# A feed-forward's products of halves: seven instead of eight, with the up-projection and the down-projection apart

## The chip, the cores and the metric

One core of a Trainium2 chip. The metric is the device time of one execution in microseconds (us); the time given for a kernel is the median of its runs.

The engines are named as in the profile: PE is TensorE (matmuls; PEld its weight loads), DVE is VectorE, ACT is ScalarE, POOL is GpSimd, SP is SyncE, which issues the DMAs. A suffix q (SPq) is an engine's own queue of DMA issues and waits.

## The reference

One layer of a streaming encoder, in float32, for 1024 tokens of a prompt and 64 tokens of a sample, 1088 columns in all: two kinds of attention, an attention into a memory, and a feed-forward with a short convolution. The change is in the feed-forward alone, and in the norm that feeds it:

```python
D_MODEL, D_FF, CONV_W = 1024, 2816, 3

def conv_ffn(h, prev, w_up, w_conv, b_conv, w_down):
    gu = h @ w_up                                   # 1024 -> 2 * 2816
    gate, val = gu[..., :D_FF], gu[..., D_FF:]
    t = gate.shape[1]
    gp = jnp.concatenate([prev.astype(gate.dtype), gate], axis=1)
    conv = sum(gp[:, j:j + t] * w_conv[j] for j in range(CONV_W)) + b_conv
    y = (jax.nn.silu(conv) * val) @ w_down          # 2816 -> 1024
    return y, gp[:, -(CONV_W - 1):]

xp = xp + mem_attend(rms_norm(xp, g_norm2), mk, mv, w_mq, g_mq, w_mo)
f, conv_p = conv_ffn(rms_norm(xp, g_norm3), zeros_prev, w_up, w_conv, b_conv, w_down)
xp = xp + f                                         # the same for the sample's xs
```

## The kernel before

All of it runs transposed: features lie on the 128 partitions, the 1088 tokens along the free axis. A float32 product is made of three matmuls: each operand is split in a high part (`hi`, a cast on ACT to a narrower float, fp32r) and a low part (`lo`, the operand less its high part, on POOL or DVE), and hi x hi, hi x lo and lo x hi are summed in PSUM (`SPLIT`).

Tokens come in three chunks (`CHUNKS`: 384, 384 and 320). `gemm` (L859) makes the products of one block of 128 outputs with one chunk in eight pieces, one for each 128 of the inner dimension, of three matmuls each (L866), in a PSUM bank named `pj`. The weights come through `Stream` (L831): halves of 128 x 512 are loaded to `raw` on SP (L840), cast to `hi` on ACT (L848) and `lo` made on POOL (L849).

The output of the memory attention goes through `project`, which adds it to the residual, stores the sum in DRAM (`x2d`, called `xd`), multiplies it by the next norm's gain into two parts (`h3`, in the slots `hhi` and `hlo`), and sums its squares; `after_mo` (its matmul is L1194) makes the reciprocal root of a chunk's mean square from those, `rstd`. It is applied behind the gate's and the value's products, and not to `h3`.

The feed-forward goes over 22 blocks of 128 features (`Tile`, L1235). `Tile.run` (L1258) makes the block's gate for the three chunks, times `rstd` on DVE into a padded row (L1269); the convolution is an ACT instruction (L1272) and two on DVE over 1090 columns (L1274), then SiLU on ACT (L1276) and `rstd` again on POOL (L1280). The value's products follow, times the gate on DVE (L1287), split in two parts on ACT (L1288) and POOL (L1289). Between the pieces of these products stand those of `Tile.down` (L1292) of the block before: for 8 blocks of outputs and 3 chunks, three matmuls each (L1298) in the banks `PT`, `O` and `tq`, added by DVE (L1305) into eight rows `y` in SBUF. The first block adds the residual (loaded at L1302), the last stores the result (L1307). The block's rows of the down-projection's weights are loaded (L1247) and split (L1255 on ACT, L1256 on POOL) in slots named `kPh` to `vSl`.

The tile framework's scheduler puts the instructions of each engine in an order and adds the waits; rows of a tile pool are reused when all readers of the earlier content are done.

Of the kernel before, what the change touches and what calls it, by code (L numbers as in the profile page):

```python
# [15 lines left out]
P = 128  # L16
# [17 lines left out]
CHUNKS = ((0, 384), (384, 384), (768, 320))  # L34


@with_exitstack
def hybrid_step(ctx: ExitStack, tc: tile.TileContext, i: dict, o: dict):
# [30 lines left out]
    def rsq(pl, ms, out, n, rows=P):  # L69
        """out = ms ** -0.5, by exp and log and one step of Newton's."""  # L70
# [8 lines left out]
    # ------------------------------------------------------------------ projections and attention  # L79
# [12 lines left out]
    ps = ctx.enter_context(tc.tile_pool(name="ps", bufs=1, space=PSUM))  # L92
# [58 lines left out]
    def load_x(c, z):  # L151
        """Half of the columns of 256 tokens, or of the sample's 64."""
# [45 lines left out]
    # K, V and Q of a pair of heads over 256 tokens  # L198
# [14 lines left out]
    def qk_norm(p, sq, raw, eps_ap, rows):  # L213
        """q and k of raw [rows, 256], each head's normed, twice in a row; k with its gain, for the cache."""
# [35 lines left out]
    def place(main, subs):  # L250
        """main, and after some of its parts others."""
# [6 lines left out]
    def proj(p, t, subs):  # L258
        """One block of tokens through a pair's columns, woven with subs; what is to be done with it later."""
# [79 lines left out]
    def forget():  # L339
        """log sigmoid of the forget logits, and their running sums."""  # L340
# [4 lines left out]
        # z = exp(-|f|); log1p(z) = log(u) - ((u - 1) - z) / u with u = 1 + z  # L345
# [1076 lines left out]
```

## Time and profile before

| | |
|---|---|
| median of 3 runs | 1879.69 us (1878.67 to 1885.91) |
| span of the profiled execution | 1878.9 us, 0.8 below the median |
| mean granted TensorE clock | 0.992 |
| PE busy | 1808.8 us, 96% of the span |
| weight loads busy | 1754.7 us, 93% |
| DVE, ACT, POOL busy | 1071.5 us (57%), 800.9 us (43%), 937.4 us (50%) |
| feed-forward, first to last matmul | 1091.7 to 1874.9 us |
| DMA over the span | 157.49 MB, 84 GB/s in the mean |

The rows of the profile read as follows. In a group, "x168 | 93.1, 554 | 92.3 <-PE PT L1298 92.3" is 168 instructions, 93.1 us busy in all, 554 ns in the mean for one, and 92.3 us for which the engine was idle just ahead of them, ended by PE's matmuls of L1298. In a row by source, "x24: 671/682/1785" is the shortest, the median and the longest in ns. A row of the timeline begins with the start and the duration in us. Matmuls overlap in the pipeline, so that the distance of two starts, not the duration, is what one more of them takes. DMA rows end with the KB of one and the median us from issue to landing; in the engines' tenths each digit is a fortieth of the span.

### The profile page before, as it was taken

The numbers are of one execution on the slowest core, as the hardware profiler recorded it, in microseconds if no ns is written. First come the engines' busy times: TensorE is split into PE (matmuls) and PEld (weight loads), VectorE is DVE, ScalarE is ACT, GpSimd is POOL, SyncE is SP. The second block draws the span as 40 slices with busy tenths as digits, with TensorE's granted clock in tenths as the row PEclk, the third lists the DMA queues.
The fourth block names the chain that finished last, engine by engine and source line by source line (L and its number), as shares of the span: only waits on it lengthen the run. The fifth ranks groups of instructions, "written<-read, shape, count | busy, mean of one in ns | idle before, by whom it ended". The sixth has DMA issues, their size and how long they took to land.

```text
span 1878.9 us, 31543 instructions
## 1 busy us (share of the span) xinstructions
PE 1808.8 (96%) x11426; PEld 1754.7 (93%) x11426; DVE 1071.5 (57%) x2537; ACT 800.9 (43%) x1828; POOL 937.4 (50%) x1312
## 2 busy tenths in 40 slices
PE   6899999999997899999999999999999999999999
PEld 5789999999996788999999999999999999999999
DVE  6777766767766875334443345445545545555546
ACT  5656666767766665335543332212212212222220
POOL 5646666877976443434433444434434434443441
PEclk9999999999998999999999999999999999999999
DMA  8312122212216776421113433111111111111102
GB/s 276 89 45 68 43 76 77 63 55 76 60 34 177 248 227 196 144 67 52 60 52 122 137 104 106 45 40 51 40 45 51 35 51 45 40 51 40 45 23 97
DMA packets 111339, 157.49 MB, mean 84 GB/s; under 512 B 15480, under 2 KB 75000, under 8 KB 111184
## 3 DMA queue, kind: packets, MB, share of 16 engines
q1 hardware_dynamic: 111184, 155.48, 26.6%
q8 instruction: 90, 1.47, 0.3%
q14 instruction: 65, 0.53, 0.1%
HBM read 125.40 MB, written 33.18 MB: 84 GB/s over the span
## 4 chain that ended last, share of the span: by engine, by line
PE 54%; POOL 1%; issue 1%; ACT 0%; DVE 0%; POOLq 0%; DVEq 0%; ACTq 0%
PE pj L866 37%; PE PT L1298 7%; PE tq L1298 3%; PE O L1298 3%; PE S L1110 1%; PE O L1146 1%; PE tq L1146 1%; POOL lo L849 1%; PE PT L1133 0%; PE O L1110 0%; PE PT L1091 0%; POOL s L1125 0%; PE PT L1194 0%; ACT hi L848 0%; PE PT L1026 0%
## 5 line engine op out<-in xcount | busy, mean ns | idle before, releaser
L866 PE MATMUL pj<-hhi,hi 128*128 128x384 f32 (+1 forms) x1248 | 412.8, 331 | 0.0
L866 PE MATMUL pj<-hlo,hi 128*128 128x384 f32 (+1 forms) x1248 | 408.8, 328 | 0.0
L866 PE MATMUL pj<-hhi,lo 128*128 128x384 f32 (+1 forms) x1248 | 408.3, 327 | 0.0
L849 POOL TENSOR_TENSOR lo<-raw,hi 128x512 fp32r<-128x512 f32 x136 | 176.9, 1302 | 336.7 <-ACT hi L848 336.0
L848 ACT CAST hi<-raw 128x512 fp32r<-128x512 f32 x136 | 84.1, 620 | 406.5 <-issue 253.0
L866 PEld LDWEIGHTS pj<-hhi,hi 128*128 128x128 f32 x1248 | 234.5, 188 | 0.5
L866 PEld LDWEIGHTS pj<-hlo,hi 128*128 128x128 f32 x1248 | 234.6, 188 | 0.1
L866 PEld LDWEIGHTS pj<-hhi,lo 128*128 128x128 f32 x1248 | 234.4, 188 | 0.1
L1305 DVE TENSOR_TENSOR a<-PT,a 128x384 f32<-128x384 f32 (+1 forms) x252 | 133.9, 531 | 158.2 <-PE PT L1298 158.2
L268 PE MATMUL pj<-whi,xhi 128*128 128x384 f32 (+1 forms) x512 | 195.5, 382 | 7.9 <-ACT xhi L126 6.7
L866 PE MATMUL pj<-a,hi 128*128 128x384 f32 (+1 forms) x736 | 183.5, 331 | 3.6 <-DVE qhi L1001 1.7
L268 PE MATMUL pj<-whi,xlo 128*128 128x384 f32 (+1 forms) x512 | 175.7, 343 | 5.9 <-DVE xlo L127 5.9
L268 PE MATMUL pj<-wlo,xhi 128*128 128x384 f32 (+1 forms) x512 | 177.2, 346 | 2.9 <-POOL wlo L119 2.9
L866 PEld LDWEIGHTS pj<-a,hi 128*128 128x128 f32 x736 | 129.4, 188 | 6.2 <-DVE a L909 2.5
L454 ACT ACTIVATE s<-s,mx 128x640 f32<-128x640 f32 (+7 forms) x128 | 94.2, 736 | 79.1 <-DVE mx L452 77.5
L491 DVE TENSOR_TENSOR ptl<-PT,pth 128x512 fp32r<-128x512 f32 (+2 forms) x192 | 99.6, 522 | 38.8 <-ACT pth L490 36.5
L866 PE MATMUL pj<-a,lo 128*128 128x384 f32 (+1 forms) x368 | 120.7, 329 | 0.0
L220 POOL TENSOR_TENSOR r<-m,mhalf 128x4 f32<-128x4 f32 (+1 forms) x72 | 73.8, 1025 | 90.0 <-DVE m L219 80.0
L268 PEld LDWEIGHTS pj<-whi,xhi 128*128 128x128 f32 x512 | 100.0, 196 | 8.9 <-ACT xhi L126 6.7
L268 PEld LDWEIGHTS pj<-whi,xlo 128*128 128x128 f32 x512 | 98.0, 191 | 6.6 <-DVE xlo L127 6.6
L268 PEld LDWEIGHTS pj<-wlo,xhi 128*128 128x128 f32 x512 | 99.6, 195 | 4.5 <-POOL wlo L119 4.5
L490 ACT CAST pth<-PT 128x512 fp32r<-128x512 f32 (+2 forms) x192 | 85.1, 449 | 38.2 <-PE PT L489 36.8
(443 smaller groups left out, 4465.2 us busy)
## 6 DMA issues: line engine op xcount, KB each, us to landing
raw<-in_w_up_dram SPq DMA_DIRECT2D x88, 256.0 KB, 2.6
kvraw<-in_w_down_dram SPq DMA_DIRECT2D x44, 256.0 KB, 2.5
wraw<-in_w_dram SPq DMA_DIRECT2D x56, 192.0 KB, 2.4
mwraw<-in_w_mkv_dram SPq DMA_DIRECT2D x16, 512.0 KB, 5.6
s<-in_xn_dram SPq DMA_DIRECT2D x8, 512.0 KB, 6.8
mixd<-mix SPq DMA_DIRECT2D x32, 128.0 KB, 1.8
bias<-negc SPq DMA_DIRECT2D x8, 512.0 KB, 3.6
raw<-in_w_o_dram SPq DMA_DIRECT2D x16, 256.0 KB, 3.5
```

Source lines behind the costliest of these rows:

```text
L220: pool.tensor_tensor(r[:rows], m[:rows], mhalf[:rows, 0:4], op=ALU.pow)
L268: pe.matmul(pj[:, :nw], x2[a][:, k, t * P:(t + 1) * P], wt[k][b][:, :nw], start=n == 0, stop=n == 3 * KT - 1)
L454: act.activation(s[:, :n], s[:, :n], ACT.Exp, bias=mx, scale=-1.0, accum_out=sm)
L490: act.copy(hi[:, f:f + n, j], pt[:, f:f + n])
L491: dve.tensor_tensor(lo[:, f:f + n, j], pt[:, f:f + n], f32(hi[:, f:f + n, j]), op=ALU.subtract)
L848: act.copy(hi, raw)
L849: pool.tensor_tensor(lo, raw, f32(hi), op=ALU.subtract)
L866: pe.matmul(out()[:, :cn], w[a][:, k % 4], x[b][k][:, c0:c0 + cn], start=k == 0 and n == 0, stop=k == KT - 1 and n == 2)
L1110: pe.matmul(sp[:rows], self.q[a][:, d, t * P:t * P + rows], k[b][:, d], start=n == 0, stop=n == 5)
L1146: pe.matmul(op[:, a0:a1], v[x][:, b, d * P:(d + 1) * P], self.p2[y][:, b, a0:a1], start=n == 0, stop=n == 5)
L1298: pe.matmul(d[:, :cn], self.wd[x][m // 4][:, (m % 4) * P:(m % 4 + 1) * P], self.a[w][:, c0:c0 + cn], start=z == 0, stop=z == 2)
L1305: dve.tensor_tensor(dst, d[:, :cn], dst, op=ALU.add)
```

## The change

Tokens are cut in two halves of 544 (`H`), and each half is one PSUM tile `W` of two banks with 272 columns in each (`Q`); there are four such tiles. The inner dimension is cut in halves too, and so are the outputs: block f goes with block f + 11 (up), or output block m with m + 4 (down). A product of two 2 x 2 matrices of such parts is then made of seven products in place of eight (one level of the Strassen-Winograd scheme), named X1, Z1, X2, Z2, Y1, Y2, Y3. Their operands are sums and differences of the quarters, and the results are sums of them: X2 is added onto X1 in X1's PSUM tile, Z2 onto Z1, Y2 and Y3 onto Y1, each after the content so far has been read.

- Up: 22 units, gate and value in turn (`Gate`, `Value`), for a pair of blocks each; a product is 4 x 2 x 3 = 24 matmuls of 272 columns (L1371). The order of the products is written out (`order`): Y1 of a unit, X1 of the next, Y2, Z1 of the next, Y3, X2 and Z2 of the next. Quarters of weights (128 x 512) are loaded two units ahead (L1255 in `Side.load`), summed on DVE (`Left.source`, L1261 to L1266) and split four products ahead (`parts_of`: ACT L1242, and L1243 on DVE for Z1, Y1, Y3, on POOL for the others).
- The right operands are made once: `h3`'s second half of tokens becomes a difference of the halves as the rows are made (`sum_of_halves`, L1226 to L1230, for which the rows of `w_mo` come in the order `ROWS`), and Y1's, Y2's and Y3's are made behind the first products (`t2`, L1381; `t34`, L1391). The third norm of the last chunk (`norm3`) is behind the first product.
- `finish` (L1475 on) evacuates the products: X1 on ACT (L1482), Z1 (L1486), Z2 (L1491), Y1 (L1493), Y2 (L1497) and Y3 (L1500) on DVE; `first` (L1421 and L1460) and `later` (L1425 and L1466, POOL) multiply by `rstd` or the gate; `conv` is as before (ACT L1434, DVE L1436, ACT L1438).
- The gated rows go to DRAM (`ad`, L1461 and L1467) and the down-projection comes after all of the up-projection: six groups of two pairs of blocks (the last of one), seven products in turn, each for four pairs of output blocks, of 2 x 2 x 3 = 12 matmuls. `load_down` loads quarters of rows and weights (L1255, into `hhi` and `hlo`), which are summed and split for the product after the running one. DVE adds the results (L1585) into `y`, loaded from `xd` at L1526; X1's are kept in `x1s` (L1578) and added by POOL to three quarters of `y` in the last group (L1581).

```diff
+H, Q = N // 2, N // 4
+ROWS = (0, 4, 1, 5, 2, 6, 3, 7)
...
+    def parts_of(hi, lo, src, e):
+        act.copy(hi, src)
+        e.tensor_tensor(lo, src, f32(hi), op=ALU.subtract)
+        return hi, lo
...
+    class Left(Side):
+        def source(self, what, e):
+            a11, a12, a21, a22 = self.q
+            if what == "Z1":
+                e.tensor_tensor(a21, a21, a22, op=ALU.add)
+            if what == "Z2":
+                e.tensor_tensor(a21, a21, a11, op=ALU.subtract)
+                e.tensor_tensor(a12, a12, a21, op=ALU.subtract)
+            if what == "Y2":
+                e.tensor_tensor(a11, a22, a21, op=ALU.subtract)
+            return {"X1": a11, "Z1": a21, "X2": a12, "Z2": a12, "Y1": a21, "Y2": a11, "Y3": a22}[what]
...
+    order = [(0, x) for x in NAMES[:4]]
+    for n in range(NF):
+        nxt = [(n + 1, x) for x in NAMES[:4]] if n + 1 < NF else []
+        order += [(n, "Y1")] + nxt[:1] + [(n, "Y2")] + nxt[1:2] + [(n, "Y3")] + nxt[2:]
...
+    def product(n, what, left, rights, c0=0, begin=True, end=True):
+        fresh = what in OPENS
+        if fresh and begin:
+            xbanks[n, what[0]] = wide_bank()
+        w = xbanks[n, what[0]]
...
+        for z in range(2):
+            for j in range(k):
+                for x, (a, b) in enumerate(SPLIT):
+                    pe.matmul(w[:, z, :Q], left(a, j), rights[j][b][:, z * Q:z * Q + Q],
...
+        if what == "Y1":
+            dve.tensor_tensor(halves(z2), w, halves(z2), op=ALU.add)
+            u.later(0, z2)
+            u.conv(0)
+        if what == "Y2":
+            dve.tensor_tensor(halves(z1), w, halves(z1), op=ALU.add)
+            u.later(1, z1)
+        if what == "Y3":
+            dve.tensor_tensor(halves(x1), w, halves(x1), op=ALU.add)
+            u.first(1, x1, pool)
+            u.conv(1)
...
+    for s, (g, what) in enumerate(steps):
+        todo = jobs(s + 1)
+        fs = groups_[g]
+        for m in range(4):
+            w = product(m, what, lambda a, j: down_ops[s, fs[j], 0][a][:, m * P:(m + 1) * P], [down_ops[s, f, 1] for f in fs])
...
+            if what == "X1":
+                if g == 0:
+                    act.copy(halves(x1s[m]), w)
                 else:
...
+                    dve.tensor_tensor(halves(x1s[m]), w, halves(x1s[m]), op=ALU.add)
+                if g == len(groups_) - 1:
+                    for dst in (y[m][:, H:N], y[m + 4][:, 0:H], y[m + 4][:, H:N]):
+                        pool.tensor_tensor(dst, dst, x1s[m], op=ALU.add)
+                continue
+            k, c = {"X2": (m, 0), "Z1": (m + 4, H), "Z2": (m, H), "Y1": (m, H), "Y2": (m + 4, H), "Y3": (m + 4, 0)}[what]
+            dst = y[k][:, c:c + H]
+            dve.tensor_tensor(halves(dst), w, halves(dst), op=ALU.add)
```

How the instructions stand on three engines follows. Names with a number are rows (`a_...`); `W`, `PT`, `O`, `tq` and `pj` are PSUM tiles.

On DVE before, in the feed-forward, the additions of the block before (L1305) stand around the convolution (L1274):

```order
L1305 TENSOR_TENSOR a_14725<-O,a_14725 128x384
L1269 TENSOR_TENSOR a_14735<-pj,ptl 128x256
L1269 TENSOR_TENSOR a_14735<-pj,ptl 128x64
L1305 TENSOR_TENSOR a_14725<-PT,a_14725 128x384
L1305 TENSOR_TENSOR a_14725<-tq,a_14725 128x320
L1274 SCALAR_TENSOR_TENSOR a_14737<-a_14735,sq,a_14737 128x1090 x2
L1305 TENSOR_TENSOR a_14726<-PT,a_14726 128x384
L1305 TENSOR_TENSOR a_14726<-O,a_14726 128x384
L1287 TENSOR_TENSOR qhi<-pj,a_14737 128x384
```

On DVE in the change, in a gate unit, from Z2's evacuation to Y3's:

```order
L1491 TENSOR_TENSOR qlo<-W,qhi 128x544
L1493 TENSOR_TENSOR qlo<-W,qlo 128x544
L1243 TENSOR_TENSOR vPl<-vSl,vPh 128x512
L1436 SCALAR_TENSOR_TENSOR a_18382<-a_14769,s,a_18382 128x1090 x2
L1497 TENSOR_TENSOR qlo<-W,qlo 128x544
L1486 TENSOR_TENSOR qlo<-W,qhi 128x544
L1243 TENSOR_TENSOR lo<-raw,hi 128x512
L1263 TENSOR_TENSOR raw<-raw 128x512
L1266 TENSOR_TENSOR raw<-kSh,raw 128x512
L1500 TENSOR_TENSOR qhi<-W,qhi 128x544
```

The convolution now stands between the evacuations of Y1 (L1493) and Y2 (L1497) of the same PSUM tile, and splits and sums of weights, which DVE did not have, between Z1's of the next unit (L1486) and Y3's (L1500).

On SP before, at the feed-forward's start, the loads of weights and of residuals:

```order
L840 DMA raw<-in_w_up_dram 128x512
L1302 DMA qlo<-x2d 128x384
L1302 DMA qlo<-x2d 128x320
L840 DMA raw<-in_w_up_dram 128x512
L1247 DMA kvraw<-in_w_down_dram 128x512
L840 DMA raw<-in_w_up_dram 128x512 x2
```

On SP in the change, where the up-projection ends, with the last stores of gated rows, the loads of `y`, and those of the down-projection:

```order
L1467 DMA ad<-a_19821 128x480
L1467 DMA ad<-a_19821 128x64
L1526 DMA a_20113<-x2d 128x1088
L1526 DMA a_20114<-x2d 128x1088
L1461 DMA ad<-a_19821 128x544
L1526 DMA a_20115<-x2d 128x1088
L1526 DMA a_20116<-x2d 128x1088
L1526 DMA a_20117<-x2d 128x1088
L1526 DMA a_20118<-x2d 128x1088
L1255 DMA hhi<-ad 128x544 x2
L1255 DMA hlo<-in_w_down_dram 128x512 x4
L1255 DMA hhi<-ad 128x544 x4
```

The residual's loads moved from the start of the feed-forward to its middle, and the first loads of the down-projection's operands are behind them and behind the last stores.

On POOL before, in the last blocks, splits and products of the gate alone:

```order
L1256 TENSOR_TENSOR vSh<-kvraw,kSh 128x512
L1280 TENSOR_TENSOR a_14736<-a_14736,pth 128x384 x2
L1280 TENSOR_TENSOR a_14736<-a_14736,ptl 128x256
L1280 TENSOR_TENSOR a_14736<-a_14736,ptl 128x64
L1289 TENSOR_TENSOR a_14731<-qhi,a_14730 128x384 x2
L849 TENSOR_TENSOR lo<-raw,hi 128x512 x2
L1289 TENSOR_TENSOR a_14731<-qhi,a_14730 128x320
```

On POOL in the change, in the last group of the down-projection:

```order
L1243 TENSOR_TENSOR kPl<-hlo,kPh 128x512
L1243 TENSOR_TENSOR a_22824<-hhi,a_22824 128x544
L1243 TENSOR_TENSOR a_22864<-hhi,a_22864 128x544
L1581 TENSOR_TENSOR a_20111<-a_20111,a_20119 128x544
L1581 TENSOR_TENSOR a_20115<-a_20115,a_20119 128x544 x2
L1581 TENSOR_TENSOR a_20112<-a_20112,a_20119 128x544
L1581 TENSOR_TENSOR a_20116<-a_20116,a_20119 128x544 x2
L1581 TENSOR_TENSOR a_20113<-a_20113,a_20120 128x544
L1581 TENSOR_TENSOR a_20117<-a_20117,a_20120 128x544 x2
L1581 TENSOR_TENSOR a_20114<-a_20114,a_20120 128x544
L1581 TENSOR_TENSOR a_20118<-a_20118,a_20120 128x544 x2
L1243 TENSOR_TENSOR a_22906<-hhi,a_22906 128x544
```

Twelve additions to `y` stand between the splits of the group's first products and those of its later ones.

More of the change, by code (lines that the diff above doesn't have):

```diff
@@ new lines, in hybrid_step, with left_place, weight_raw @@
+    lefts = [0]
+    def left_place():
+        n = lefts[0] % 7
+        lefts[0] += 1
+        if n < 4:
+            return [stream.pl.tile([P, 4, P], F32R, name=x, bufs=4).rearrange("p k c -> p (k c)") for x in ("hi", "lo")]
+        return [tmp(x, [P, 2, 256]).rearrange("p a b -> p (a b)") for x in (("vPh", "vPl"), ("kPh", "kPl"), ("kvraw", "kvraw"))[n - 4]]
+    def weight_raw(n):
+        if n % 2 == 0:
+            r = [lambda: stream.pl.tile([P, 4, P], F32, name="raw", bufs=3).rearrange("p k c -> p (k c)")] * 3
+            return r + [lambda: row("kSh", 512)]
+        return [lambda x=x: row(x, 512) for x in ("kSl", "vSh", "vSl", "sq")]
@@ L1211, in hybrid_step @@
+    AHEAD = 4
     last = attending(mems[-1], mems[-2])
-    for n, g in enumerate(project(32, oT, ORDER, [], x1d, xd, h3, 2, ("kPh", "kPl", "kSh"), after_mo)):
+    for n, g in enumerate(project(32, oT, ORDER, ROWS, [], x1d, xd, h3, 2, [row("kPh"), row("kPl"), early_x], after_mo,
+                                  lambda m: m > 3 and sum_of_halves(m - 4))):
         subs = [(at - 8 * n, f) for at, f in last if 0 <= at - 8 * n < 8] + take()
@@ new lines, in hybrid_step @@
+    nc.sync.dma_start(o["conv"], cv)
+    DOWN = ("X1", "X2", "Z1", "Z2", "Y1", "Y2", "Y3")
+    groups_ = [range(a, min(a + 2, NF // 2)) for a in range(0, NF // 2, 2)]
+    steps = [(g, what) for g in range(len(groups_)) for what in DOWN]
+    big = [f32(hb.tile([P, KT, N], F32R, name=x)).rearrange("p k t -> p (k t)") for x in ("hhi", "hlo")]
+    y = [f32(arow(n)) for n in (4, 5, 6, 7, 8, 9, 14, 15)]
+    x1s = [r[:, z * H:z * H + H] for r in (f32(arow(10)), f32(arow(11))) for z in range(2)]
```

334 lines of the change are left out of this document (236 added, 98 removed).

## The prediction

> **What bounds the kernel now.** I read the first page, then the chain that ended last, then busy time by stretch, then single instructions.
>
> ```profile
> span 1878.9 us, 31543 instructions
> PE 1808.8 (96%) x11426; PEld 1754.7 (93%) x11426; DVE 1071.5 (57%) x2537; ACT 800.9 (43%) x1828; POOL 937.4 (50%) x1312
> PE   6899999999997899999999999999999999999999
> PE 54%; POOL 1%; issue 1%; ACT 0%; DVE 0%; POOLq 0%; DVEq 0%; ACTq 0%
> PE pj L866 37%; PE PT L1298 7%; PE tq L1298 3%; PE O L1298 3%; PE S L1110 1%; PE O L1146 1%; PE tq L1146 1%; POOL lo L849 1%; PE PT L1133 0%; PE O L1110 0%; PE PT L1091 0%; POOL s L1125 0%; PE PT L1194 0%; ACT hi L848 0%; PE PT L1026 0%
> ```
>
> TensorE is the bound; the chain is made of the matmuls of L866 (up-projection, earlier projections) and L1298 (down-projection). The stretches (from:to, length, then busy time of PE, weight load, DVE, ACT, POOL, granted clock, DMA share, GB/s) show where it is not: a dip at the third norm, and none in the feed-forward.
>
> ```profile
> 1050.00:1100.00 50.00, 47.45 (x280) 45.81 (x279) 19.52 (x34) 20.04 (x37) 24.70 (x25) 1.00 0.41 129
> 1091.70:1874.60 782.90, 782.82 (x4725) 782.51 (x4724) 408.75 (x750) 161.42 (x238) 311.49 (x364) 1.00 0.16 52
> ```
>
> So the feed-forward is 783 us of unbroken matmuls, and DVE and POOL have half their time free. Only fewer or shorter matmuls shorten it, and any wait that a new order brings to PE adds its full length.
>
> **What is removed: one product in eight.** Before, 22 blocks x 2 x 8 pieces x 3 x 3 chunks = 3168 matmuls up and 22 x 24 x 3 = 1584 down, 4752, two thirds of 384 columns and one third of 320. After, 22 units x 7 x 24 = 3696 up, and 11 pairs of blocks x 7 x 4 x 2 x 3 = 1848 down: 5544 of 272 columns. What one costs is the distance of starts in an unbroken run:
>
> ```profile
> 1400.14 0.34 PE L866 MATMUL pj<-hhi,hi 128*128 128x384 f32 x1
> ...
> 1402.05 0.34 PE L866 MATMUL pj<-hhi,lo 128*128 128x384 f32 x1
> 1412.14 0.31 PE L866 MATMUL pj<-hhi,hi 128*128 128x320 f32 x1
> ...
> 1412.87 0.31 PE L866 MATMUL pj<-hhi,lo 128*128 128x320 f32 x1
> 827.26 0.28 PE L1110 MATMUL S<-kPh,qhi 128*128 128x256 f32 x1
> 827.98 0.34 PE L866 MATMUL pj<-hhi,hi 128*128 128x384 f32 x1
> ```
>
> 384 columns: 1.91 us over 11 steps, 0.174. 320: 0.73 over 5, 0.146. 256: six of them in 0.72, 0.120. On the line between the last two, 272 columns take 0.1265 us, and 5544 of them 701; the ends are 665 (at 0.120) and 809 (at 0.146). Against 783 I take -82.
>
> The Trainium skill, "TensorE: Matmul & The Clock Gate", section "Back-to-back issue gap", gives columns / 2.4 + 2.5 ns for an isolated matmul, 116 ns for 272, and by it the 5544 would take 642 us. It gives 162.5 ns for 384, where the rows above show 174, so the measurement decides.
>
> **What hides the rest, and where it no longer does.** Each product now must be evacuated before another is added onto its PSUM tile (X2 onto X1, Z2 onto Z1, Y2 and Y3 onto Y1), and the sums of quarters are DVE and POOL work. Prices:
>
> ```profile
> L1305 DVE TENSOR_TENSOR a<-PT,a 128x384 f32<-128x384 f32 x168 | 93.1, 554 | 92.3 <-PE PT L1298 92.3
> L491 DVE TENSOR_TENSOR ptl<-PT,pth 128x512 fp32r<-128x512 f32 x72 | 49.4, 690 | 19.0 <-ACT pth L490 18.9
> L706 DVE TENSOR_TENSOR kclo<-kraw,kchi x24: 671/682/1785, 622.0 to 705.2; 128x512 fp32r<-128x512 f32 x24
> L1274 DVE SCALAR_TENSOR_TENSOR a<-a,sq,a x44: 1354/1364/2285, 1100.8 to 1847.1; 128x1090 f32<-128x1090 f32 x44
> L849 POOL TENSOR_TENSOR lo<-raw,hi 128x512 fp32r<-128x512 f32 x100 | 129.5, 1295 | 318.7 <-ACT hi L848 318.3
> L1280 POOL TENSOR_TENSOR a<-a,pth 128x384 f32<-128x384 f32 x44 | 43.7, 1014 | 27.1 <-ACT a L1276 27.1
> L1280 POOL TENSOR_TENSOR a<-a,ptl 128x64 f32<-128x64 f32 x22 | 6.6, 301 | 0.0
> L848 ACT CAST hi<-raw 128x512 fp32r<-128x512 f32 x100 | 62.0, 620 | 395.1 <-issue 253.0 <-PE pj L866 140.8 <-POOL kPl L1011 1.1
> L1272 ACT ACTIVATE a<-a,sq 128x1090 f32<-128x1090 f32 x22 | 28.7, 1304 | 18.5 <-DVE a L1269 16.8
> ```
>
> By their slopes 544 columns cost DVE 0.725 from PSUM (0.554 at 384, 0.690 at 512) and 0.71 from SBUF (0.68 at 512); POOL 1.37 (1.014 at 384, 1.295 at 512). There is a further price, for DVE with two SBUF inputs beside POOL:
>
> ```profile
> 1165.36 3.66 DVE L1274 SCALAR_TENSOR_TENSOR a<-a,sq,a 128x1090 f32<-128x1090 f32 x2 [0.45 <-ACT a L1272]
> 1165.91 1.95 POOL L1256 TENSOR_TENSOR vSh<-kvraw,kSh 128x512 fp32r<-128x512 f32 x1 [0.34 <-ACT kSh L1255]
> L601 DVE TENSOR_TENSOR mwlo<-mwraw,mwhi x16: 673/1126/1780, 578.4 to 691.2; 128x512 fp32r<-128x512 f32 x16
> L706 DVE TENSOR_TENSOR kclo<-kraw,kchi 128x512 fp32r<-128x512 f32 x24 | 19.2, 814 | 1.7 <-ACT kchi L705 1.5
> ```
>
> The pair of L1274 alone takes 2 x 1.36 = 2.72; here 3.66, while POOL's 1.30 became 1.95: the one waits for the other's instruction to end. So such an instruction of DVE waits 0.13 us in the mean at L706 (814 against 682), 0.45 in the median at L601 (1126 against 673), 0.91 at the worst L1274 (2285 against 1364).
>
> *Start of the up-projection.* The products of unit 0 stand ahead; behind X1 come the norm of the last chunk, the right-hand sums of Y1 (L1381), then those of Y2 and Y3 (L1391). DVE has some 20 instructions ahead of Z1's evacuation (L1486), 13.8 us at 0.71, while PE has 10.5 us of work; with the waits for POOL PE stands 6.6 us. The next 13.5 us ahead of L1493 cost 6.5 more. The dip of before, 50 - 47.45 = 2.5, goes. +10; range 3 (DVE without waits, half of it behind evacuations) to 15.
>
> *Inside the up-projection.* The tight link is Y1's end to Y3's start in a gate unit: L1493 0.725, POOL's L1425 1.22 + 0.30, L1434 1.30, two L1436 2.72, L1497 0.725 = 7.0, with hand-overs 7.4, against three products of 24 x 0.1265, 9.1. Waits of 0.5 to 1.15 for POOL fit in most units; 11 gate units at half a microsecond: +6, range 0 to 25 (every pair of L1436 at the worst wait, and L1243 ahead of it). The other load does fit: POOL 16.9 and DVE's two-input work 10.3 exclude each other, 27.2 us in a gate unit, 14.6 in a value unit, 41.8 against 42.6 of PE for both. The weights of two units ahead are covered as before: 2.6 us to land, 21 us early.
>
> *Seam from up to down.* It is the one place without other products to run: Y1, Y2, Y3 of the last unit follow each other, so their evacuations show, +3. Then the last gated rows must go to DRAM and come back:
>
> ```profile
> raw<-in_w_up_dram SPq DMA_DIRECT2D x88, 256.0 KB, 2.6
> x2d<-qhi SPq DMA_DIRECT2D x16, 192.0 KB, 1.9
> 10.00:20.00 10.00, 5.73 (x20) 5.55 (x21) 7.20 (x13) 4.34 (x10) 8.09 (x10) 1.00 1.06 347
> 578.00:582.00 4.00, 0.58 (x1) 0.29 (x1) 1.18 (x3) 3.95 (x9) 3.92 (x7) 0.59 0.27 84
> 582.00:586.00 4.00, 2.42 (x10) 2.04 (x11) 3.88 (x9) 2.00 (x6) 1.66 (x2) 0.50 0.85 240
> 586.00:590.00 4.00, 3.77 (x17) 3.48 (x18) 3.01 (x6) 2.96 (x6) 3.78 (x6) 0.50 0.84 301
> ```
>
> On SP the loads of y (L1526) stand ahead of the down-projection's loads (L1255), and some of y's rows come free only as unit 21 ends. Behind them lie 2.4 MB, 7 us at the 347 GB/s of the third row; then a cast, 0.62, and POOL's 1.37. The store's 1.9, the loads, and L1493 to L1467 before them make PE idle some 15. After such an idle the fourth and fifth row show a clock of 0.59 and 0.50; 4 us at half speed cost 2. +20; range 8 (loads early, only the store waits) to 25.
>
> *Down-projection.* Per group of two pairs PE has 7 x 4 x 12 x 0.1265 = 42.7 us. DVE has 28 evacuations, 20.3, and 24 two-input instructions at 0.69, 16.6: 36.9 without waits. POOL has 26.9, so it is busy 63% of the time; at a mean wait of 0.35 (between L706 and L601, nearer the busier L601) DVE needs 45.3, 2.6 more than PE, and with 5 such groups and their first steps +15. Ends: 0, if waits fall between evacuations; 80, at 0.91 each (58.7 a group). DVE passes PE at (42.7 - 36.9) / 24 = 0.24.
>
> *Last group.* One pair, so PE has 21.3 us, but POOL gets twelve adds of x1 to y (L1581), 16.4 us, behind its splits, and as Z1's evacuations write the same quarters of y, they wait for them; two wide tiles stay taken meanwhile, and PE stands. DVE then has 20 evacuations in a row:
>
> ```profile
> 1874.92 0.48 DVE L1305 TENSOR_TENSOR a<-tq,a 128x320 f32<-128x320 f32 x1
> ```
>
> Before, the end lies 1878.9 - 1875.4 = 3.5 behind the last evacuation, and that stays. The last evacuation moves from 22 to 32 us behind the group's start. +10, range 8 to 20.
>
> Hidden: the sums of halves of h3 (L1226) run beside w_mo's products, where DVE has 30 of 50 us free; the copy of X1 (L1482) runs on ACT, which is busy 161 of 783 us.
>
> **The sum.** -82 + 10 + 6 + 20 + 15 + 10 = -21: span 1858. The run of the profile lies 0.8 below the median of 1879.69, so I give 1858.
>
> **Rivals.**
> *The waits are hidden* (0.15): all terms at or little above their low ends, 3 + 2 + 8 + 5 + 8 = 26, 1823. For it: in the down-projection DVE has 36.9 of work in 42.7 us, and a wait that falls between two evacuations costs nothing. Against: there are four PSUM tiles, so PE runs at most three products ahead of an evacuation.
> *No measurable change* (0.15): waits of 0.5 in the down-projection (36.9 + 12 = 48.9, 6.2 a group, 31) beside a start of 12, 6 within, a seam of 25 and a last group of 8 make 82: 1879. For it: L601's median of 0.45. Against: it needs three terms near their upper ends at once.
> *DVE becomes the bound of the down-projection* (0.16; the other side): every two-input instruction meets POOL as the worst L1274 does, 0.91. 58.7 against 42.7 is 80 a stage, 65 more than forecast: 1923. With the other terms as summed (46), it turns the gain into a loss from (36 / 5 + 5.8) / 24 = 0.54 us a wait on, little above L601's median. Against: L706's 0.13.
> The Trainium skill, "SBUF — State Buffer", section "Who interferes with whom", says that a DVE instruction with two SBUF inputs contends with a GpSimd one that reads SBUF, that the lock lasts the whole instruction and the other fully blocks. The rows of 1165.36 agree (3.66 for 2.72).
> *Shorter matmuls are no cheaper* (0.02): at 0.146 each 809 instead of 701, 1965. Against: six of 256 columns at 0.120.
>
> **How the numbers follow.** The forecast has 0.52, between 1838 and 1870 by its own terms. About 0.5%, 9 us, is what a measurement of this kernel can tell from no change. Faster: forecast and the first rival, 0.67; same 0.15; slower 0.18. The range of 1825 to 1895 takes in the unchanged case and most of the forecast's terms at both ends; it leaves out the worst waits and half of the hidden case.
>
> **What would show it.** Starts of 272-column matmuls 0.1265 apart; PE gaps at the first units with L1486 and L1493 as releasers; nearly none between; a hole of 15 us at the seam, ended by POOL's or DVE's split of a quarter from `ad`, followed by a clock near 0.5; in the down-projection gaps ended by L1585, with L1243 and the sums on DVE well above 0.69. It is wrong if waits per two-input instruction exceed 0.54 us, if the seam takes over 30, or if gaps recur in every gate unit.

## The result: 1% slower

The changed kernel takes 1898.88 us in the median of four runs (1897.33 to 1901.4), the kernel before 1879.63; the ratio is 1.009, with a 95% interval of 1.0067 to 1.0113. The forecast was 1858, range 1825 to 1895, faster at 0.67.

The first page of the changed kernel, and its chain:

```profile
span 1896.6 us, 33871 instructions
PE 1742.5 (92%) x12218; PEld 1675.2 (88%) x12218; DVE 1264.2 (67%) x2456; ACT 889.1 (47%) x1980; POOL 1176.2 (62%) x1428
PE   6899999999996899999999879999999997699997
PEclk9999999999998999999999979999999998799999
PE 25%; DVE 11%; POOL 10%; issue 5%; DMA 4%; ACT 2%; SPq 0%; POOLq 0%; DVEq 0%; ACTq 0%
```

PE is busy 66 us less than before (1808.8), and the span is 17.7 longer: it now waits 154 us in all, where it waited 70. Before, DVE had no share in the chain and POOL 1%; now DVE has 11% and POOL 10%. The slices have three dips that were not there before: the 23rd and 24th (the feed-forward's start), the 34th and 35th (the seam) and the last.

The stretches of the feed-forward (from:to, length, busy time of PE, weight load, DVE, ACT, POOL, clock, DMA share, GB/s): start, up-projection, seam, five groups down, last group.

```profile
1088.50:1160.00 71.50, 53.24 (x350) 51.06 (x351) 65.13 (x66) 26.26 (x40) 49.76 (x42) 0.83 0.10 37
1160.00:1589.00 429.00, 413.01 (x3291) 411.14 (x3290) 267.44 (x290) 132.49 (x191) 302.52 (x309) 1.00 0.20 69
1589.00:1640.00 51.00, 26.03 (x160) 24.61 (x160) 24.39 (x26) 13.97 (x24) 26.32 (x20) 0.70 0.80 285
1640.00:1851.00 211.00, 197.90 (x1529) 192.04 (x1528) 196.28 (x234) 71.58 (x128) 139.00 (x91) 1.00 0.22 72
1851.00:1897.00 46.00, 31.63 (x224) 29.85 (x222) 31.05 (x43) 5.32 (x9) 27.32 (x19) 0.90 0.26 98
```

An undisturbed run of 272-column matmuls has its starts 0.125 apart, here 13 steps in 1.63 us (the rows between are left out):

```profile
1179.76 0.29 PE L1371 MATMUL W<-hhi,lo 128*128 128x272 f32 x1
...
1181.39 0.28 PE L1371 MATMUL W<-hhi,hi 128*128 128x272 f32 x1
```

So 5544 of them take 693 us, and what a stage takes beyond 0.125 for each matmul is its loss. Summed over the trace, with the part that is half clock (starts 0.227 apart) in brackets:

| | forecast | measured |
|---|---|---|
| matmuls, against 783 before | -82 | -90 |
| start: 27.6 [5.8], less 3.1 by which its first matmul is earlier | +10 (3 to 15) | +24.5 |
| inside the up-projection | +6 (0 to 25) | +18.0 [0.5] |
| seam | +20 (8 to 25) | +31.2 [4.3] |
| down-projection, five groups | +15 (0 to 80) | +20.1 [3.0] |
| last group | +10 (8 to 20) | +13.2 [2.2] |
| sum | -21 | +17 |

What ended PE's waits, from the view of waits, first in the start, then the up-projection, the seam, and the down-projection with its last group:

```profile
PE W L1371 <- POOL lo L1243: 7.2, 1, 7.2
PE W L1371 <- ACT qhi L1482: 5.7, 2, 4.8
PE W L1371 <- DVE qlo L1493: 3.2, 1, 3.2
...
PE W L1371 <- DVE qlo L1493: 15.8, 9, 1.8
...
PE W L1371 <- ACT a L1242: 20.8, 2, 18.5
...
PE W L1371 <- DVE a L1585: 18.0, 24, 2.9
PE W L1371 <- DVE a L1578: 4.6, 5, 1.0
```

Each row gives the sum, the times and the longest. The up-projection's loss is one wait, nine times the same; of the seam's 31.2, 18.6 are one hole. The 3.1 in the start's row is no more than scatter: the feed-forward's first matmul lies at 1088.6 in this trace, and between 1089.2 and 1093.9 in four others whose edits lie behind it.

### The profile page after: what moved, and what is told of

The parts are those of the page before. It is cut to its first block, busy times and chain, and to the rows that moved or that the text cites. A ratio compares the mean times of both kernels' runs of the same rounds, so it can differ in the third digit from the quotient of the medians.

```text
span 1896.6 us, 33871 instructions
## 1 busy us (share of the span) xinstructions
PE 1742.5 (92%) x12218; PEld 1675.2 (88%) x12218; DVE 1264.2 (67%) x2456; ACT 889.1 (47%) x1980; POOL 1176.2 (62%) x1428
## 4 chain that ended last, share of the span: by engine, by line
PE 25%; DVE 11%; POOL 10%; issue 5%; DMA 4%; ACT 2%; SPq 0%; POOLq 0%; DVEq 0%; ACTq 0%
PE W L1371 12%; PE pj L868 9%; POOL a L1425 2%; DVE a L1585 2%; POOL a L1441 1%; DMA kSh<-in_w_up_dram 1%; DVE a L1436 1%; DMA hhi<-ad 1%; POOL kPl L1243 1%; POOL a L1243 1%; ACT a L1434 1%; POOL a L1439 1%; POOL a L1421 1%; POOL a L1581 1%; PE S L1115 1%
## 5 line engine op out<-in xcount | busy, mean ns | idle before, releaser
L1371 PE MATMUL W<-a,hi 128*128 128x272 f32 x1040 | 204.7, 292 | 40.1 <-ACT a L1242 20.8
L1371 PEld LDWEIGHTS W<-a,hi 128*128 128x128 f32 x1040 | 165.0, 191 | 44.7 <-ACT a L1242 21.2
L1371 PE MATMUL W<-hhi,lo 128*128 128x272 f32 x536 | 156.4, 292 | 8.7 <-POOL lo L1243 7.2
L1371 PE MATMUL W<-hhi,hi 128*128 128x272 f32 x536 | 156.7, 292 | 6.0 <-ACT qhi L1482 5.7
L1243 POOL TENSOR_TENSOR a<-hhi,a 128x544 fp32r<-128x544 f32 x77 | 119.4, 1569 | 62.4 <-ACT a L1242 62.4
L1371 PE MATMUL W<-hlo,hi 128*128 128x272 f32 x536 | 156.2, 292 | 0.0
L1371 PE MATMUL W<-a,lo 128*128 128x272 f32 x520 | 150.8, 290 | 0.0
L1371 PE MATMUL W<-a,kvraw 128*128 128x272 f32 x792 | 121.5, 297 | 20.8 <-DVE qlo L1493 19.0
L1371 PEld LDWEIGHTS W<-a,kvraw 128*128 128x128 f32 x792 | 109.4, 196 | 24.4 <-ACT vPh L1242 17.5
L1436 DVE SCALAR_TENSOR_TENSOR a<-a,s,a 128x1090 f32<-128x1090 f32 x44 | 72.6, 1650 | 72.6 <-ACT a L1434 72.2
L1585 DVE TENSOR_TENSOR a<-W,a 128x544 f32<-128x544 f32 x144 | 99.9, 713 | 16.7 <-POOL a L1581 8.4
L1371 PEld LDWEIGHTS W<-hhi,lo 128*128 128x128 f32 x536 | 102.5, 191 | 9.2 <-POOL lo L1243 7.5
L1371 PE MATMUL W<-a,vPh 128*128 128x272 f32 x528 | 104.7, 291 | 5.3 <-DVE a L1585 5.3
```

Of the source, the lines that this page charges most:

```text
L1243: e.tensor_tensor(lo, src, f32(hi), op=ALU.subtract)
L1371: pe.matmul(w[:, z, :Q], left(a, j), rights[j][b][:, z * Q:z * Q + Q], start=fresh and begin and j == 0 and x == 0, stop=final and end and ...
L1436: dve.scalar_tensor_tensor(t[:, 0:N + 2], gp[:, j:N + 2 + j], cw[:, f, j:j + 1], t[:, 0:N + 2], op0=ALU.mult, op1=ALU.add)
L1585: dve.tensor_tensor(halves(dst), w, halves(dst), op=ALU.add)
```

## The experiments

Line numbers are those of the changed kernel; where an edit adds lines, an experiment's own rows count a few more. Losses of a stage are what the starts of the same matmuls take in each run beyond 0.125 each: the first 349 of the feed-forward for the start (28.0 in the changed kernel, as the norm's own matmul lies between them), then 3289 up (17.9), 158 at the seam (31.2), 1527 down (20.1) and the last 220 (13.3).

### One suspected wait at a time

**Seam.** The first two pairs of the down-projection are loaded ahead of the last unit's Y products, and `y` behind them:

```diff
     for g, (n, what) in enumerate(order):
+        if g == len(order) - 3:
+            load_down(0)
+            load_down(1)
...
-    for m in range(8):
-        nc.sync.dma_start(y[m][:, :N], xd[m])
     for f in jobs(0):
         f()
+    for m in range(8):
+        nc.sync.dma_start(y[m][:, :N], xd[m])
```

> The down-projection's first two pairs are loaded ahead of the last unit's Y products and of the loads of y. Theory 1 (SP takes its queue in order: 2.2 MB of y and the last stores stand ahead of the rows that PE waits for): the hole of 18.8 us at the seam falls to 3 to 8, time about 1886. Theory 2 (the hole is the transfer itself, or the round trip of the last gated rows through DRAM): it stays above 15, time 1896 to 1899.

1889.7 us, ratio 1.0039 (1.0025 to 1.0053): 9.6 us less than the change. In the changed kernel SP's queue and PE stood like this:

```profile
1607.68 0.32 SPq L1461 DMA_DIRECT2D ad<-a  x1
1608.09 2.14 SPq L1526 DMA_DIRECT2D a<-x2d  x4
1610.29 1.30 SPq L1255 DMA_DIRECT2D hhi<-ad  x2
1611.63 2.38 SPq L1255 DMA_DIRECT2D hlo<-in_w_down_dram  x4
1615.23 3.09 SPq L1255 DMA_DIRECT2D hhi<-ad  x4
1625.40 0.82 PE L1371 MATMUL W<-a,hi 128*128 128x272 f32 x2 [18.47 <-ACT a L1242]
```

PE has done the three matmuls that the first pair's rows allow and stands for the second pair's (`hhi<-ad` of 1615.23). Those are in DRAM long before, but their load stands behind the store of the last unit's rows, four loads of `y`, and the rest of the first pair. With the loads ahead the hole of 18.8 us is gone; two of 2.8 and 3.7 are left, and the stage's loss falls from 31.2 to 17.2, with 2.8 more in the groups behind it. So the hole is the late load, as theory 1 said, with a gain 3 us smaller. The run does not tell the queue's order from the transfers: it also issues the loads before the last unit's Y products, which then hide them, and in the changed kernel the DMA engines are full from 1609 to 1627 (a share of 0.98 to 1.06 in every 3 us).

**Up-projection.** In gate units the multiplication behind Y3 is made by DVE:

```diff
-            u.first(1, x1, pool)
+            u.first(1, x1, dve if n % 2 == 0 else pool)
```

> The gate's multiplication of the second half behind Y3 (L1421) on DVE in place of POOL, in gate units alone. Theory 1 (the 2.03 us that PE waits once in two units are a chain from Y3 through POOL's queue, ACT and the convolution on DVE to the next unit's Y1 evacuation, which stands behind the convolution in DVE's order; the chain becomes some 3 us shorter): the ten gaps go, -18, time 1880. Theory 2 (the sum of DVE's and POOL's work on their common port is the bound in the up-projection): the gaps stay at 1.5 or more, time 1893 to 1900.

1881.81 us, ratio 0.9998 (0.9983 to 1.0012): 17 us less, theory 1. The loss of the stage falls from 17.9 to 5.1, and the view of waits has 1.0 left of the 15.8 (the other 4 to 5 us lie in the start and the seam, 3 and 2 less, which the edit does not explain):

```profile
PE W L1371 <- DVE qlo L1493: 1.0, 3, 0.4
```

The chain is seen in one unit of the changed kernel (PE, DVE, POOL and ACT in order of time; the first row is the last matmul of Y3):

```profile
1361.62 0.28 PE L1371 MATMUL W<-a,lo 128*128 128x272 f32 x1
1362.71 0.69 DVE L1266 TENSOR_TENSOR raw<-kSh,raw 128x512 f32<-128x512 f32 x1
1363.32 0.72 DVE L1500 TENSOR_TENSOR qhi<-W,qhi 128x544 f32<-128x544 f32 x1
1366.66 1.36 POOL L1421 TENSOR_TENSOR a<-qhi,ptl 128x544 f32<-128x544 f32 x1
1368.05 1.30 ACT L1434 ACTIVATE a<-a,s 128x1090 f32<-128x1090 f32 x1 [5.57 <-POOL a L1421]
1369.39 1.35 DVE L1436 SCALAR_TENSOR_TENSOR a<-a,s,a 128x1090 f32<-128x1090 f32 x1 [4.35 <-ACT a L1434]
1374.80 0.71 DVE L1493 TENSOR_TENSOR qlo<-W,qlo 128x544 f32<-128x544 f32 x1
1375.66 2.61 PE L1371 MATMUL W<-a,kvraw 128*128 128x272 f32 x19 [1.76 <-DVE qlo L1493]
```

From the end of Y3's matmuls to the end of Y1's evacuation in the next unit 13.6 us pass, while PE has four products of 3.0 to do; then Y2 waits. Y3's evacuation (L1500) begins 1.4 late, behind sums of weights. L1421 begins 2.6 late, as POOL still has L1425 and a split; DVE stands idle for 4.35 in front of L1436 with the evacuations behind it.

**Down-projection without POOL.** Low parts by a second copy on ACT:

```diff
-        down_ops[s, f, side] = parts_of(*place(), src, e)
+        if e is pool:
+            hi, lo = place()
+            act.copy(hi, src)
+            act.copy(lo, src)
```

> Left out in the down-projection: POOL's splits; their low parts are copies of the sources made on ACT, so POOL has nothing to do there until the last group's adds. DVE's own work is the same. Theory 1 (DVE's instructions with two SBUF inputs wait for POOL, 0.46 us each in the mean, and this alone makes DVE the bound): these instructions fall to 0.67 to 0.72, gaps of PE in the down-projection from 20 + 13 to under 10 in all, time about 1877. Theory 2 (four PSUM tiles and DVE's own 36.9 us in bursts make the gaps): gaps stay above 20, time above 1888.

The kernel leaves out the subtraction, so its low parts are plain copies. It takes 1872.89 us in its one run, and in 200 us of the down-projection PE does not wait once:

```profile
1640.00:1840.00 200.00, 200.00 (x1605) 200.00 (x1604) 160.05 (x246) 126.83 (x231) 1.72 (x2) 1.00 0.24 74
```

Its splits on DVE, by source (shortest, median and longest in ns):

```profile
L1243 DVE TENSOR_TENSOR lo<-hlo,hi x22: 681/684/748, 1597.3 to 1828.3; 128x512 fp32r<-128x512 f32 x22
```

DVE's instructions with two SBUF inputs are back at 0.68 to 0.72; in the changed kernel 106 of them took 121 us in the same stage, 1.14 each, a wait of 0.46. DVE has 160 us in 200 without these waits and 196 in 211 with them. Theory 1: four PSUM tiles are enough, and DVE's own work is not the bound. The run takes POOL's part in the splits away with its port, and both go together; but in the changed kernel all waits of PE in this stage are ended by DVE's evacuations (L1578, L1585) and none by a split on POOL, which speaks for the port.

**Last group.** Only the order of the twelve adds:

```diff
-                if g == len(groups_) - 1:
-                    for dst in (y[m][:, H:N], y[m + 4][:, 0:H], y[m + 4][:, H:N]):
-                        pool.tensor_tensor(dst, dst, x1s[m], op=ALU.add)
+                if g == len(groups_) - 1 and m == 3:
+                    for k, c in ((4, H), (0, H), (4, 0)):
+                        for q in range(4):
+                            dst = y[q + k][:, c:c + H]
+                            pool.tensor_tensor(dst, dst, x1s[q], op=ALU.add)
```

> Only the order of POOL's twelve adds in the last group (L1581) is changed: those to the quarters that Z1's evacuations write come first, then Z2's, then Y3's. Theory 1 (three of Z1's evacuations wait for adds to other quarters that stand ahead of theirs on POOL, and PE with them): the two gaps of 3.1 us and one of 1.4 go, -6 to -8, time about 1892. Theory 2 (the last group is bound by DVE's evacuations or POOL's 16 us in all): gaps come back behind the reordered adds, time above 1896.

1890.97 us, ratio 1.005 (1.0034 to 1.0067): 7.5 us less, theory 1, and the loss of the last group falls from 13.3 to 5.4. In the changed kernel, DVE's evacuations of Z1 waited like this for POOL, and that is gone:

```profile
1863.53 16.17 POOL L1581 TENSOR_TENSOR a<-a,a 128x544 f32<-128x544 f32 x12
1875.87 0.72 DVE L1585 TENSOR_TENSOR a<-W,a 128x544 f32<-128x544 f32 x1 [3.15 <-POOL a L1581]
1879.74 3.27 DVE L1585 TENSOR_TENSOR a<-W,a 128x544 f32<-128x544 f32 x5 [3.15 <-POOL a L1581]
```

### The start: order or amount

**First order.** On ACT the copy of X1 ahead of the casts of Y1's sums (`issue_after` puts a block behind an instruction in its engine's queue), and the splits of Y2's and Y3's sums on DVE:

```diff
-        parts_of(right(what, 0, j), right(what, 1, j), u, pool)
+        parts_of(right(what, 0, j), right(what, 1, j), u, dve)
...
+            with tc.issue_after(evac[0]):
                 for j in range(4):
                     t2(j)
```

> On ACT the copy of X1 of unit 0 (L1482) is put ahead of the casts of the right-hand sums of Y1, and the splits of the sums of Y2 and Y3 (t34) are made on DVE, not POOL. Theory 1 (PE waits at the start for work that stands in an in-order queue behind other waits: 5.1 us on ACT, 7.5 us behind five splits on POOL): both gaps shrink, -8 to -12, time 1887 to 1891. Theory 2 (DVE is the bound of the start, all in all): the waits turn up at other products, time within 3 of 1899.

1897.69 us, ratio 1.0088 (1.007 to 1.0107): no change, theory 2, though the start's loss in its trace is 24.6. The two waits went (4.8 to 1.1, 7.2 to 2.8) and others came: 6.2 in front of the norm's matmul, and 5.9 for Y1's evacuation.

**Second order.** X1, Z1, X2, Z2 on PE, and the sums of Y1's right side behind the norm, the evacuation and the last sum of squares:

```diff
+            with tc.issue_after(evac[0]), tc.issue_after(marks['norm']), tc.issue_after(marks['acc']):
                 for j in range(4):
                     t2(j)
```

> Order alone, at the start: PE takes X1, Z1, X2, Z2 of unit 0 in this order (X2 stood second, onto a tile that was not yet evacuated), and on DVE, ACT and POOL the right-hand sums of Y1 stand behind the norm of the second chunk, the evacuation of X1 and the last sum of squares. All work stays. Theory 1 (half of the start's loss is the order: the sums stand ahead of the norm's chain and of X1's evacuation): gaps and half clock of 1088 to 1160 fall from 27.6 to 12 to 20, time 1886 to 1894. Theory 2 (DVE's work and its waits for POOL are the bound, order only moves the gaps, as in the first try): over 24 stay, time 1896 or more.

1900.62 us, ratio 1.0108 (1.0087 to 1.0129): no better than the change, theory 2; 27.2 lost in the start. The norm's wait fell to 1.1, and PE waited 8.4 for a split of unit 1's weights behind those of the sums on POOL.

**Without the sums.** `t2` and `t34` split rows of `h3` as they are, and the sums are left out:

```diff
-        e.tensor_tensor(t, f32(h1), f32(l1), op=ALU.add)
-        e.tensor_tensor(t, f32(h2_), t, op=ALU.subtract)
-        e.tensor_tensor(t, f32(l2), t, op=ALU.add)
-        parts_of(right("Y1", 0, j), right("Y1", 1, j), t, e)
+        parts_of(right("Y1", 0, j), right("Y1", 1, j), h1, e)
```

> Left out: the sums and differences of the right-hand sides of Y1, Y2 and Y3 (L1381 to L1383, L1391 to L1397); rows of h3 are split in their place, in the same splits on the same engines. Theory 1 (DVE is the bound of the start: some 25 sums, and their waits for POOL): gaps and half clock between 1088 and 1160 fall from 27.6 to under 12, time 1882 or less. Theory 2 (the order of single instructions on ACT, PE and POOL holds PE, whatever DVE has to do): over 20 stay.

1887.32 in its one run, 14.0 lost in the start in place of 28.0, between the 12 of theory 1 and the 20 of theory 2. Of that, 7.3 is one wait in front of the norm's matmul, which is 0.5 in the changed kernel. The edit makes it: without sums the splits on POOL are ready early and stand ahead of the last sum of squares (L1014), for which the norm waits:

```profile
1094.07 7.83 POOL L1243 TENSOR_TENSOR a<-hhi,a 128x544 fp32r<-128x544 f32 x5
1101.86 1.31 POOL L1014 TENSOR_TENSOR x<-x,qlo 128x320 f32<-128x320 f32 x1
```

Beside that wait 6.7 are left, so the sums make at least half of the loss, and most of it if the 7.3 belongs to the edit alone. DVE is busy for 28.0 of the start's first 41.5 us here, and for 40.4 in the changed kernel. This run takes POOL's three sums away too.

**Both orders together.**

> Both changes of order of the start together: norms and evacuation first, X1, Z1, X2, Z2 in this order on PE, and the eight splits of Y2's and Y3's sums on DVE, so that none stands on POOL ahead of the weights of unit 1 (the 8.4 us that PE waited for POOL in the run with norms first). Theory 1 (order): 12 to 18 of gaps and half clock between 1088 and 1160, time 1884 to 1892. Theory 2 (DVE's amount of work): over 22, the waits at the sums of Y2 and Y3, time 1894 or more.

1901.37 us, ratio 1.01 (1.0078 to 1.0121), 26.6 lost: theory 2. The longest wait left, and under it the first 41.5 us of the start:

```profile
PE W L1374 <- DVE qlo L1499: 11.2, 2, 8.0
```

```profile
1088.50:1130.00 41.50, 29.11 (x187) 27.28 (x186) 38.53 (x53) 13.20 (x23) 13.81 (x10) 0.83 0.06 20
```

The same stretch of the changed kernel:

```profile
1088.50:1130.00 41.50, 27.96 (x180) 26.62 (x181) 40.35 (x42) 13.21 (x23) 25.73 (x16) 0.79 0.04 12
```

DVE is busy for 38.5 and 40.4 of 41.5 us. In the changed kernel it does 42 instructions in that time, 0.96 each, as POOL holds it up; with the splits on DVE 53, 0.73 each: fewer waits and more work. Counted from the first matmul, Y1's first evacuation (L1493, here L1499) begins after 41.8 us in the changed kernel, after 37.7, 40.5 and 39.8 in the three orders, and after 28.0 without the sums. With the order alone PE's waits go from one releaser to the next, and most of the sum stays.

### Joined

**combo1**: the seam's order, L1421 on DVE, the last group's order, and the first two pairs' weights loaded two units ahead in the up-projection's own slots:

```diff
+    ups += [Left(weight_raw(n), down_quarters(n - NF)) for n in (NF, NF + 1)]
...
-        if what == "Y3" and n + 2 < NF:
+        if what == "Y3":
             ups[n + 2].load()
```

> Together: the seam's loads ahead of those of y, the first two pairs' weights of the down-projection loaded two units ahead in the up-projection's slots, the gate's L1421 on DVE, and the adds of the last group in the order of Z1, Z2, Y3. Theory 1 (each is an independent wait of PE): 1899 - 9.6 - 17 - 7 and 3 to 6 more at the seam, 1860 to 1866, under the kernel before. Theory 2 (port and DVE take it back): 1872 or more.

1852.32 us, ratio 0.9855 (0.9834 to 0.9875): below both kernels, and below the 1860 to 1866 of theory 1. The single gains add up to 34, this is 44 below the change; with the weights ahead the seam loses 8.0, where the seam's order alone left 17.2.

**combo2** has all splits of weights of the up-projection on DVE beside that:

```diff
-        e = dve if what in ("Z1", "Y1", "Y3") else pool
+        e = dve
```

> As the one before, and all splits of weights of the up-projection on DVE (POOL has 8 fewer of 1.30 us in two units, DVE 8 more of 0.68). Theory 1 (POOL and DVE exclude each other, so 5 us of shared time in two units fewer): what is left of gaps in the up-projection, 6.8, falls to 0 to 3, time 3 to 6 less than the one before. Theory 2 (DVE is the nearer bound, its evacuations stand behind more work): gaps grow, time the same or up to 20 more.

1858.02 us, 0.9879 (0.9864 to 0.9894), 4.5 us more than combo1 by the ratios, with intervals that overlap: not theory 1. The loss of the up-projection grows from 4.9 to 11.8, as theory 2 said. POOL has 178 of 410 us in place of 294, and yet Y1's evacuation is late again, 0.9 nine times:

```profile
PE W L1376 <- DVE qlo L1498: 8.4, 9, 1.5
```

**combo3** is combo1 with three pairs in a group of the down-projection (and a third pair loaded at the seam), and **combo4** has the splits of Z2's and Y2's weights on DVE beside that:

```diff
-    groups_ = [range(a, min(a + 2, NF // 2)) for a in range(0, NF // 2, 2)]
+    groups_ = [range(a, min(a + 3, NF // 2)) for a in range(0, NF // 2, 3)]
...
-        e = pool if side or what in ("X2", "Z2", "Y2") else dve
+        e = pool if side or what == "X2" else dve
```

> The first combination (1852.3), with groups of three pairs in the down-projection (3, 3, 3, 2): 112 evacuations in place of 168, with the same sums, splits and matmuls; only one of three pairs can be loaded well ahead. Theory 1 (DVE is the bound there with its waits, so 56 evacuations of 0.71, 40 us less on it, free it): the 23 us of gaps of the down-projection fall to 5 to 12, time 1838 to 1846. Theory 2 (the common port is the bound: sums 0.69 and POOL's splits 1.33 add up to 65 in 63 us for a group whatever the evacuations): 15 or more stay, or loads late at the groups' seams, time 1847 or more.

> As the one before, and the splits of Z2's and Y2's weights in the down-projection on DVE, not POOL (22 of 88 of POOL's). Theory 1 (port): 13 us less of shared time over the stage, which DVE can take since it has fewer evacuations: 3 to 8 less than the one before. Theory 2 (DVE is still the nearer bound): the same or slower.

1868.91 (0.994, 0.9922 to 0.9957) and 1856.03 (0.9883, 0.9857 to 0.991). combo3 is 16 us slower than combo1, theory 2 by its time: the first 1527 matmuls down lose 21.1 in place of 23.1, the seam 12.5 in place of 8.0, the last group 15.9 in place of 5.4. So a third of the evacuations less gained 2 us where it was to gain 11 or more. The shifted splits then gained 10.7 us (a ratio of 0.0057, with intervals apart), 6.7 of it in those 1527. That fits the shared port as the limit there, and not DVE's evacuations; these two runs alone do not show it. Both had a new hole of 10 to 12 us in the last group, in whose place two pairs now stand: splits of its products stood behind twelve adds on POOL.

**combo5** is combo1 with the second order of the start: 1853.96, 0.9858 (0.9843 to 0.9873): no gain, theory 2 of the start.

> The first combination (1852.3) with the start in the order of norms first. By theory 1 of the start: 1840 to 1846. By theory 2: 1850 or more.

**combo6** and **combo7** are combo4 with the second order of the start and the adds spread between the splits; combo7 has the eight splits of the start on DVE too:

```diff
+            if g == len(groups_) - 1 and what in ("X2", "Y1"):
+                late = y[m][:, H:N] if what == "X2" else y[m + 4][:, 0:H]
+                with tc.issue_after(marks2[3] if what == "X2" else marks3["Y1"]):
+                    pool.tensor_tensor(late, late, x1s[m], op=ALU.add)
```

> Groups of three pairs with the splits of Z2's and Y2's weights on DVE (1856.0), with the last group's adds spread (four each ahead of Z1, Z2 and Y3, splits of later products between them) and norms first at the start. The hole of 10 us in the last group came from splits behind twelve adds: it falls under 3, time 1843 to 1849. If the adds only move the hole, 1852 or more.

> As the one before, with the eight splits of the start on DVE. By theory 1 of the start 8 us less than the one before, 1836 to 1842; by theory 2 the same within 3.

1853.19 (0.9841, 0.982 to 0.9863) and 1848.91 (0.9823, 0.9806 to 0.984). combo6 missed its range and came out at the 1852 or more of the other reading: the hole went to waits of up to 3.4, the last group loses 6.5 in place of 12.6, but the seam 14.1 in place of 10.1, and why is open. combo7 has the lowest time here, 1.8% under the kernel before and 2.6% under the change; its interval overlaps with combo1's. It is 4.3 below combo6, with intervals that overlap: half of what theory 1 of the start asked, a little more than theory 2 allowed. Its up- and down-projection:

```profile
1155.00:1565.00 410.00, 408.13 (x3253) 406.26 (x3252) 266.05 (x299) 134.23 (x192) 292.52 (x299) 1.00 0.24 78
1620.00:1808.00 188.00, 178.11 (x1381) 177.04 (x1380) 166.07 (x194) 63.03 (x114) 114.40 (x72) 0.97 0.24 78
```

It still loses 24.4 at the start, 12.5 at the seam, 15.7 in the first 1527 matmuls down (one wait of 2.4 to 2.5 in the middle of each group of three pairs, one of 3.4, and the half clock behind them), and 6.6 in the last 220.

## Why the prediction was wrong, step by step

The prediction named three signs of being wrong, and two of them came: the seam takes over 30 (31.2), and gaps recur in the gate units (nine of eleven).

**Matmuls, -82.** Right, and 8 us too careful: 0.125 measured for 0.1265. The formula of the Trainium skill, "TensorE: Matmul & The Clock Gate", section "Back-to-back issue gap", gives an estimate of 0.116 and 642 us in all; the trace has 0.125 and 693.

**Inside the up-projection, +6.** The failed step is the choice of the tight link. The prediction took Y1's end to Y3's start, and that fits in every unit, as it said. The link from Y3 to the next unit's Y2 was not counted: it goes over POOL, ACT and DVE, and in DVE's queue Y1's evacuation stands behind a convolution that waits for ACT, 13.6 us against 12.0 of products. Of 17.9 the one edit of L1421 took away 12.8.

**Start, +10.** The failed step is the size, and the releasers. Some 27 us of DVE were counted at 0.71 each, with 6.6 and 6.5 us of stall. DVE needed 40: 42 instructions of 0.96, as POOL's splits of the same sums stand beside its own. The stalls were ended by POOL's and ACT's queues (8.7 and 5.7) more than by DVE's L1493 (3.2), and never by L1486; the copy of X1, which the prediction called hidden on ACT, ended 5.7 of them. Four runs tell the order of these queues from the work: without the sums the loss is half, with three other orders it stays at 24.6 to 27.2.

**Seam, +20.** The mechanism was right (SP's order, `y` ahead), the size was not: 18.6 in place of 15 for the hole, 8.3 in place of 3 for the Y products and the first steps, 4.3 in place of 2 for the clock. The 15 counted 2.4 MB behind the loads of `y`, and had no term for the 2.2 MB of the four loads of `y` that SP issued just ahead of them.

**Down-projection, +15, and last group, +10.** Right in mechanism and near in size: 20.1 and 13.2. The wait for an instruction with two SBUF inputs was 0.46, not 0.35, at the upper of the two rows it was taken between (0.45); the run without POOL and the one with the adds in another order confirm both causes. In the working 336 matmuls of 0.1265 are 42.5 us, not 42.7, which moves the term by 1 us.

**The rivals.** None came as told. DVE as the bound of the down-projection asked for 0.54 a wait; it was 0.46. The loss came from three terms that each exceeded the forecast, two of them their own range: start and seam together are 25.7 of the 38.6 us between forecast and span, the up-projection 12, against 8 that the matmuls were cheaper. The prediction put these terms near the middle of their ranges. In the start and the up-projection the change gives DVE and POOL more to do at once, in queues that PE now depends on at every product; the seam's hole is another cause, loads that come late.

## What to carry to other kernels

Where a change makes the bound engine's products depend on evacuations one by one, list for each product every evacuation it needs, and walk the queue of the evacuating engine back from it, over the neighbours' work too: the tight link was between units, not within one. Add up DVE's two-input work and POOL's as one resource for each stage before trusting either's share of busy time. And a phase boundary costs what its load queue holds ahead of the first needed bytes: load those first, or in the earlier phase's own slots.

## What the runs showed of the hardware

The clock drops after short waits. After the 4.8 us of 1093.06 to 1098.14 matmuls start 0.227 apart:

```profile
1093.06 0.29 PE L1371 MATMUL W<-hhi,lo 128*128 128x272 f32 x1
1098.14 0.59 PE L1371 MATMUL W<-hhi,hi 128*128 128x272 f32 x1 [4.79 <-ACT qhi L1482]
1098.53 0.43 PE L1371 MATMUL W<-hlo,hi 128*128 128x272 f32 x1
1098.75 0.43 PE L1371 MATMUL W<-hhi,lo 128*128 128x272 f32 x1
```

A shorter wait was followed by it as well, with matmuls 0.227 apart from 1089.21 to 1092.39:

```profile
1087.49 0.91 PE L1199 MATMUL PT<-kPl,ones 128*128 128x384 f32 x2 [2.04 <-POOL kPl L1014]
1089.21 0.43 PE L1371 MATMUL W<-hlo,hi 128*128 128x272 f32 x1
1089.44 0.43 PE L1371 MATMUL W<-hhi,lo 128*128 128x272 f32 x1
```

This cost 15.7 us in the changed kernel, in 156 matmuls. The length of the wait alone does not decide: it came after 2.04 here, after 2.33 at the seam and after 3.19 in the start, but not after 2.54 in front of 1079.61, nor after the waits of 1.8 in the up-projection. The Trainium skill, "TensorE: Matmul & The Clock Gate", section "What's actually happening", gives 1.2 GHz after an idle window of some 3.4 us; 272 columns at that rate are 227 ns, which agrees, while a wait of 2.04 was enough here.

Where one of POOL's splits meets an instruction of DVE with two SBUF inputs, both take longer, as in the start of the changed kernel; 0.71 and 1.37 are what these take alone:

```profile
1110.24 1.69 POOL L1243 TENSOR_TENSOR a<-qhi,a 128x544 fp32r<-128x544 f32 x1 [9.06 <-ACT a L1242]
1110.64 1.88 DVE L1392 TENSOR_TENSOR qlo<-qlo,hlo 128x544 f32<-128x544 f32 x1
1113.28 1.72 POOL L1243 TENSOR_TENSOR a<-qlo,a 128x544 fp32r<-128x544 f32 x1 [1.34 <-ACT a L1242]
1113.71 1.87 DVE L1392 TENSOR_TENSOR qhi<-qhi,hlo 128x544 f32<-128x544 f32 x1
```
